# A hybrid decoder layer on one core: sums of weight quarters computed early on VectorE and kept in DRAM, weight units of four blocks

## The chip, the cores and the metric

The kernel runs on one core of a Trainium2 chip. The metric is the device time of one execution in microseconds; a profile of one further execution shows what every engine did.

## What is computed

One layer of a causal decoder, for 512 prompt rows and 8 x 4 sample rows together (544 token columns, all in float32):

```python
z = rmsnorm(x, g) @ w_in               # 2048 -> 7728: pooling input, queries, keys/values, gates
A = pool_mixer(...); B = nsa(...)      # windowed means; three-branch attention
h = x + rmsnorm(w_out(sigmoid(ga) * A @ w_pool_proj + sigmoid(gb) * B @ w_nsa_proj))
y = h + rmsnorm(ConvFFN(rmsnorm(h)))   # w_up: 2048 -> 2 x 5632, conv + gelu gate, w_down: 5632 -> 2048
```

## The kernel before

All weights lie in DRAM in the order of use, cut into blocks of 128 x 128. `plan()` lists the units: eight blocks each (1024 columns, 512 KB). The class `Weights` streams them. `load` brings a unit into a ring of three raw tiles by a DMA on SP's queue; `split` turns it into a high part (a copy on ScalarE, L227) and a low part (a subtraction on VectorE, L229), two halves of 512 columns each, into rings of three. `unit` (L349 to L351) multiplies: for every block and token half three matmuls of 128 x 128 by 272 columns (high by high, high by low, low by high). After these three it calls `ws.progress`, which emits the split of the unit two ahead at fixed points, and `tick(0.5)`, so a tick is six matmuls. The schedule is manual: each engine and each DMA queue works through its instructions in the order in which this program emits them.

`tick` also drives side work. A generator in `bg` takes `rate` steps per tick; attention (`compress_stage`, `natural_stage`, `sample_stage`, `prompt_stage`) is emitted this way between the matmuls of the input projection. `later` delays single actions by some ticks.

The order of the stages: a first projection of three column blocks; the columns m = 3 to 20 (keys, values, queries; background rate 0.7); 30 gate columns (rate 1.0) beside attention; the pooling columns; the merge, in which for each of 16 m the products `pp` and `np` are multiplied with gates read back from DRAM (`sg_d`); the output projection `wo`, at whose end the normalised state is formed; then the feed-forward part.

The up projection of the feed-forward part is a 2 x 2 block product in seven multiplications. Its weight matrix has four quarters per column block j (44 of these): quarters 0 and 1 belong to one row of the 2 x 2 scheme, 2 and 3 to the other. A first stage (`p`, L1383) does two of the seven products and stores them in `stash_d`. The second, called the sum stage here, does five per j: four need the sums s1 = q2 + q3, s2 = s1 - q0, s3 = q0 - q2, s4 = q1 - s2 as weights, one needs q3 itself. GpSimd computes the four sums per j (`weight_sum`, L1335, 128 x 1024 each), driven by `hooks` of the weight stream which also fetch the quarters (`quarter`, L205). The sum stage has five evacuations per j on VectorE (L1466 to L1477) and the convolution and gate (`conv`): two steps on VectorE (L1413, L1414), a gelu on ScalarE (L1415), the product with the value half on VectorE (L1418, L1419) and a store of `act_d` (L1422). The products t2 and t3 use one PSUM bank one after the other: t3 may begin once L1466 has read t2. The down projection (`dn`) follows in seven chunks.

Evacuations in the input projection use two PSUM banks, one for each token half (`pair(..., 0)`).

Of the kernel before, what the change touches and what calls it, by code (L numbers as in the profile page):

```python
# [40 lines left out]
KH = KT // 2  # L41

# [9 lines left out]
def kinner(mat, m, kts=None, halves=BOTH):  # L52
    kts = list(range(KT) if kts is None else kts)
    return [(tuple((mat, k, m) for k in kts[i:i + 8]), halves) for i in range(0, len(kts), 8)]


def kouter(mat, ms):
    return [(tuple((mat, k + i, m) for i in range(2) for m in ms), BOTH) for k in range(0, KT, 2)]


def grp(gs):
    return [(tuple(("grp%d" % g, k, m) for g in gs for m in range(2) for k in range(2)), BOTH)]


def plan():
    u = kouter("in", [0, 1, 2])
    for m in range(3, 21):
        u += kinner("in", m)
    for m in GATES[:30]:
        u += kinner("in", m)  # L70
    for m in range(8):
        u += kinner("in", M_POOL + m)
        if m == 6:
            u += grp((0, 1))
    for m in GATES[30:]:
        u += kinner("in", m)
    u += grp((2, 3))
    for m in range(KT + 1):
        if m < KT:
            u += kinner("pp", m, range(8))  # L80
        if m:
            u += kinner("np", m - 1, range(8))
    for m in range(KT - NSPLIT):
        u += kinner("out", m)
    for h in BOTH:
        for m in range(KT - NSPLIT, KT):
            u += kinner("out", m, halves=(h,))
    for j in range(0, FT, 2):
        u += [(quad(i, q), (0,)) for q in (0, 1) for i in (j, j + 1)]
    for j in range(FT):  # L90
        u += [(quad(j, q), (0,)) for q in ("s2", "s1", "s3", 3, "s4")]
    for a, b in CHUNKS:
        if b - a == 8:
            for m in range(KT):
                u += kinner("dn", m, range(a, b))
        else:
            for hs in (BOTH,) if b < FT else ((0,), (1,)):
                for m in range(0, KT, 2):
                    u += [(tuple(("dn", k, m + i) for i in range(2) for k in range(a, b)), hs)]
    return u  # L100


def quad(j, q):


    if isinstance(q, str):
        return tuple((q, k, j) for k in range(KH))
    return tuple(("up", q % 2 * KH + k, (FT if q < 2 else 0) + j) for k in range(KH))


def computed(b):
    return b[0][0][0] == "s"


def stored(units):
    return [b for b, _ in units if not computed(b)] + [quad(j, 2) for j in range(FT)]
# [58 lines left out]
class Weights:  # L175


    RAW, PARTS = 3, 3

    def __init__(self, nc, pool, dram, units):  # L180
        self.nc, self.pool, self.dram, self.units = nc, pool, dram, units
        self.i = self.nd = self.ns = 0
        self.raw, self.done = {}, {}
        self.ahead, self.depth = 1, 1
        self.off, _ = offsets(units)
        self.kept, self.again = {}, {}
        self.given, self.hooks = set(), {}
# [4 lines left out]
    def load(self, n):  # L192
        while self.nd < min(n, len(self.units)):
            if self.nd in self.again or self.nd in self.given:
# [3 lines left out]
            t = self.pool.tile([P, 1024], F32, name=f"wr{i}", tag="wraw", bufs=self.RAW)  # L198
            self.fetch(t, self.units[i][0])
            self.raw[i] = t  # L200
            self.nd += 1

    def fetch(self, t, blocks):
        w, o = len(blocks) * P, self.off[blocks]
        self.nc.sync.dma_start(t[:, :w], self.dram[o:o + P * w].rearrange("(p c) -> p c", c=w))  # L205

    def split(self, i, part):

        if i in self.again:
            if part == 0:  # L210
                self.done[i] = self.kept[self.again[i]]
            elif part == 3:
                self.ns = i + 1
            return
        if part == 0 and i in self.kept:
            self.load(i + 1)
            self.done[i] = self.kept[i]
        elif part == 0:
            self.load(i + 1)
            self.done[i] = (self.pool.tile([P, 1024], F32R, name=f"wh{i}", tag="whi", bufs=self.PARTS),  # L220
                            self.pool.tile([P, 1024], F32R, name=f"wl{i}", tag="wlo", bufs=self.PARTS))
        hi, lo = self.done[i]
        w = self.width(i)
        c = slice(0, w // 2) if part < 2 else slice(w // 2, w)
        raw = self.raw[i]
        if part % 2 == 0:
# [3 lines left out]
        if part == 3:  # L230
# [3 lines left out]
    def finish(self, i):  # L234
        while self.ns <= i:
            for part in range(4):
                self.split(self.ns, part)

    def get(self):
# [3 lines left out]
        for f in self.hooks.pop(i, ()):  # L243
            f()
        self.load(i + 1 + self.depth)
        return self.units[i] + self.done.pop(i)

    def progress(self, n, total):
# [3 lines left out]
        at = [max(1, total // 8), 3 * total // 8, total // 2, 3 * total // 4]  # L252
        if n in at:
# [4 lines left out]
            if part == 3:  # L258
                self.load(self.i + 1 + self.depth)
# [3 lines left out]
def layer(ctx: ExitStack, tc: tile.TileContext, a: dict):  # L263
# [16 lines left out]
    wp, wp_es = pool("weights", "left")  # L280
    up, up_es = pool("u", "left")
# [3 lines left out]
    ws = Weights(nc, wp, a["wst"], plan())  # L285
# [19 lines left out]
    bg = {"gen": None, "credit": 0.0, "rate": 0.0}  # L305
    deferred = []

    def tick(x=1.0):
# [4 lines left out]
        if bg["gen"] is None:  # L313
            return
        bg["credit"] += bg["rate"] * x
        while bg["credit"] >= 1.0 and bg["gen"] is not None:
            bg["credit"] -= 1.0
            if next(bg["gen"], "end") == "end":
                bg["gen"] = None

    def drain():
        while bg["gen"] is not None:
            if next(bg["gen"], "end") == "end":
                bg["gen"] = None
        while deferred:
            deferred.pop(0)[1]()

# [37 lines left out]
    def full(mat, m, ps, X, done=None):  # L365
        for _ in range(2):
# [89 lines left out]
    for k in range(0, KT, 2):  # L456
# [3 lines left out]
        ws.load(k // 2 + 2)  # L460
# [12 lines left out]
        if k == KT - 2:  # L473
            ws.ahead, ws.depth = 2, ws.RAW
            ws.finish(9)
# [3 lines left out]
        unit(lambda mat, m: psA[m], U, lambda k: k == 0, lambda k: k == KT - 1, byk=True)  # L479
# [633 lines left out]
    def grp_unit(gs):  # L1113
# [19 lines left out]
        unit(psof, X, lambda k: k == 0, lambda k: k == 1, done)  # L1133
# [44 lines left out]
    for m in range(KT + 1):  # L1178
        if m < KT:
            ga = gates[m][0]  # L1180
            p1 = pair(f"pp{m}", 2 * m)
            unit(lambda *_: p1, AX_, lambda k: k == 0, lambda k: k == 7, lambda m, h: V.scalar_tensor_tensor(
                ga[:, HS[h]], ga[:, HS[h]], 1.0, p1[h], OP.add, OP.mult))
        if m:
            ga, gb = gates.pop(m - 1)
            p2 = pair(f"np{m - 1}", 2 * m + 1)
            unit(lambda *_: p2, OX, lambda k: k == 0, lambda k: k == 7, lambda m, h: V.scalar_tensor_tensor(
                gb[:, HS[h]], gb[:, HS[h]], 1.0, p2[h], OP.add, OP.mult))
# [8 lines left out]

    v0p, v0_es = pool("v0", "right")
# [114 lines left out]
    drain()  # L1313
    mg_es.close()

    GE = 2 + SEQ + NB * 6
    ffn, raws = {}, {}
    first_sum = ws.i + 2 * FT

    def open_ffn():  # L1320
# [6 lines left out]
        ffn["fw"], ffn["fw_es"] = pool("quarters", "left")  # L1327

    def quarter(j, q, bufs=1):
        t = raws[j, q] = ffn["fw"].tile([P, 1024], F32, name=f"wq{q}_{j}", tag=f"q{q}", bufs=bufs)  # L1330
        ws.fetch(t, quad(j, q))
# [5 lines left out]
    def hook(i, f):  # L1337
        ws.hooks.setdefault(i, []).append(f)

    def give(j, b):  # L1340


        def fetch():
            quarter(j, 3, 2)
            quarter(j, 2)
            quarter(j, 0)
            ws.raw[b + 3] = raws[j, 3]

        def s1():
            weight_sum(j, "s1", 2, 3, OP.add)  # L1350
            ws.raw[b + 1] = raws[j, "s1"]

        def s2():
            weight_sum(j, "s2", "s1", 0, OP.subtract)
            ws.raw[b] = raws[j, "s2"]
            quarter(j, 1)

        def s3():
            weight_sum(j, "s3", 0, 2, OP.subtract)
            ws.raw[b + 2] = raws[j, "s3"]  # L1360

        def s4():
            weight_sum(j, "s4", 1, "s2", OP.subtract)
            ws.raw[b + 4] = raws[j, "s4"]

        for x, f in ((-6, fetch), (-4, s1), (-3, s2), (-2, s3), (0, s4)):
            hook(b + x, f)
        ws.given.update(range(b, b + 5))

    for j in range(FT):  # L1370
        give(j, first_sum + 5 * j)
# [3 lines left out]
    for j in range(0, FT, 2):  # L1375
        pa = [psp.tile([P, 512], F32, name=f"p1_{i}", tag=t, bufs=2)[:, :H2] for i, t in ((j, "g"), (j + 1, "tr"))]
        st = {}
        for q in range(2):
            for i in range(2):
                unit(lambda *_: [pa[i]], VX, lambda k: k == 0, lambda k: k % KH == KH - 1, skip=True)  # L1380
# [72 lines left out]
    for j in range(FT):  # L1453
# [3 lines left out]
        def product(ps, form, start):  # L1457
            xh, xl = forms[form]
            unit(lambda *_: [ps], lambda mat, k, h: (xh[:, k % KH, :], xl[:, k % KH, :]),
                 lambda k: start and k % KH == 0, lambda k: k % KH == KH - 1, skip=True)  # L1460
# [24 lines left out]
    ffn["fw_es"].close()  # L1485
# [42 lines left out]
    for ci, (c0, c1) in enumerate(CHUNKS):  # L1528
        first, last = (lambda k: k == c0), (lambda k: k == c1 - 1)
        if ci + 1 < len(CHUNKS):  # L1530
# [8 lines left out]
            step = 1 if c1 - c0 == 8 else 2  # L1539
            for m0 in range(0, KT, step):  # L1540
                pss = {m: nextpair(f"dn{ci}_{m}") for m in range(m0, m0 + step)}
                unit(lambda mat, m: pss[m], DX, first, last, done)
# [7 lines left out]
        for n in range(2, 8):  # L1550
            i = ws.i + n
            ws.kept[i] = tuple(kp.tile([P, 1024], F32R, name=f"k{t}{n}") for t in "hl")
            ws.again[i + 8] = i
        for h in range(2):
            for m0 in range(0, KT, 2):
                pss = {m: bank(f"dn{h}_{m}", m, h) for m in (m0, m0 + 1)}
# [25 lines left out]
    y_es.close()  # L1582
    ps_es.close()
# [95 lines left out]
```

## Time and profile before

| | |
|---|---|
| time, median of 3 runs | 3064.67 us (3063.96 to 3066.19) |
| the profiled execution | 3064.26 us, span of its instructions 3062.6 us |
| busy: TensorE, VectorE, ScalarE, GpSimd | 2906.9, 1962.4, 1101.6, 694.9 us |
| moved by DMA | 431.06 MB, 141 GB/s on average |

Busy time is the sum over an engine's instructions, with overlaps counted once. Matmuls are pipelined, so TensorE's rate is better read from the number of matmuls in a stretch than from its busy time. A DMA's time to landing runs from its issue to its last byte; issuing alone takes the queue about 0.4 us.

### The profile page before, as it was taken

Reading aid. Unit: us, or ns where it says so; the run is one execution under the profiler, and the core shown is the slowest. Engines: PE = TensorE matmul, PEld = TensorE weight load, DVE = VectorE, ACT = ScalarE, POOL = GpSimd, SP = SyncE. Lnnn points to the kernel's source line nnn. Section 1 sums busy time; section 2 is a strip of 40 time slices with the busy share of each in tenths; the row PEclk is TensorE's granted clock in tenths of the full one; section 3 lists DMA queues with packets and bytes.
Section 4 is the critical chain, followed back from the end, with each engine's and each line's share of the span. In section 5 each row is a group of like instructions: output and inputs, shape, how many; then the busy total and the mean of one; then the engine's idle time right before and its main releaser. Section 6 shows DMA issues by size and latency. Waiting matters only on the chain.

```text
span 3062.6 us, 56964 instructions
## 1 busy us (share of the span) xinstructions
PE 2906.9 (95%) x22799; PEld 2811.3 (92%) x22799; DVE 1962.4 (64%) x3353; ACT 1101.6 (36%) x2345; POOL 694.9 (23%) x576
## 2 busy tenths in 40 slices
PE   9799999999999999998999989888888899999996
PEld 9798889999999999997999988888888899999996
DVE  7232435777755544258774899999999973444347
ACT  4111224444432322245564443343444343222223
POOL 4232220000003000112100555555555520000004
PEclk9899999999999999999999999999999999999998
DMA  6542564222225443256766544444444443333234
GB/s 207 134 134 98 194 230 147 68 74 77 78 71 99 132 136 127 87 160 192 260 224 232 177 140 150 156 149 140 140 155 156 147 161 118 108 111 111 97 103 150
DMA packets 185288, 431.06 MB, mean 141 GB/s; under 512 B 39611, under 2 KB 77916, under 8 KB 185022
## 3 DMA queue, kind: packets, MB, share of 16 engines
q1 hardware_dynamic: 161240, 395.94, 38.8%
q10 hardware_dynamic: 16614, 14.68, 2.2%
q0 software_dynamic: 7168, 16.79, 1.8%
q8 instruction: 179, 2.93, 0.4%
q14 instruction: 87, 0.71, 0.1%
HBM read 369.23 MB, written 58.11 MB: 140 GB/s over the span
## 4 chain that ended last, share of the span: by engine, by line
PE 73%; DVE 17%; issue 5%; DMA 2%; ACT 1%; POOL 0%; SPq 0%; DVEq 0%; ACTq 0%; POOLq 0%
DVE wl L229 8%; PE in L349 7%; PE in L351 7%; PE in L350 6%; PE dn L351 5%; PE dn L349 5%; PE dn L350 5%; DVE cv L1413 4%; PE p L349 3%; PE p L351 3%; PE p L350 3%; PE wo L351 2%; PE wo L349 2%; PE wo L350 2%; PE oa L990 1%
## 5 line engine op out<-in xcount | busy, mean ns | idle before, releaser
L229 DVE TENSOR_TENSOR wl<-wr,wh 128x512 fp32r<-128x512 f32 (+1 forms) x756 | 542.5, 730 | 327.6 <-ACT wh L227 318.5
L227 ACT CAST wh<-wr 128x512 fp32r<-128x512 f32 (+1 forms) x756 | 439.4, 616 | 790.7 <-PE dn L350 329.5
L349 PE MATMUL in<-uh,wh 128*128 128x272 f32 x1600 | 490.5, 307 | 0.0
L351 PE MATMUL in<-uh,wl 128*128 128x272 f32 x1600 | 462.6, 289 | 0.0
L350 PE MATMUL in<-ul,wh 128*128 128x272 f32 x1600 | 461.5, 288 | 0.0
L351 PE MATMUL dn<-h,wl 128*128 128x272 f32 x1312 | 379.6, 289 | 0.0
L349 PE MATMUL dn<-h,wh 128*128 128x272 f32 x1312 | 378.3, 288 | 0.7 <-ACT y L1535 0.4
L229 DVE TENSOR_TENSOR wl<-ws,wh 128x512 fp32r<-128x512 f32 x352 | 375.0, 1094 | 4.9 <-ACT wh L227 3.4
L350 PE MATMUL dn<-l,wh 128*128 128x272 f32 x1312 | 377.2, 288 | 0.0
L349 PEld LDWEIGHTS in<-uh,wh 128*128 128x128 f32 x1600 | 302.2, 189 | 39.0 <-issue 37.9
L1335 POOL TENSOR_TENSOR ws<-wq,wq 128x1024 f32<-128x1024 f32 x88 | 225.1, 2557 | 349.3 <-PE p L351 207.2
L350 PEld LDWEIGHTS in<-ul,wh 128*128 128x128 f32 x1600 | 303.3, 190 | 0.7
L351 PEld LDWEIGHTS in<-uh,wl 128*128 128x128 f32 x1600 | 301.9, 189 | 0.2 <-DVE wl L229 0.2
L227 ACT CAST wh<-ws 128x512 fp32r<-128x512 f32 x352 | 205.5, 620 | 256.0 <-PE ug L350 94.8
L349 PEld LDWEIGHTS dn<-h,wh 128*128 128x128 f32 x1312 | 247.0, 188 | 1.1 <-ACT y L1535 0.6
L350 PEld LDWEIGHTS dn<-l,wh 128*128 128x128 f32 x1312 | 247.3, 188 | 0.0
L351 PEld LDWEIGHTS dn<-h,wl 128*128 128x128 f32 x1312 | 246.6, 188 | 0.0
L1537 DVE TENSOR_TENSOR y<-y,dn 128x272 f32<-128x272 f32 x160 | 70.1, 438 | 247.9 <-PE dn L351 247.9
L349 PE MATMUL p<-vh,wh 128*128 128x272 f32 x704 | 204.5, 290 | 0.8 <-ACT st L1383 0.8
L351 PE MATMUL p<-vh,wl 128*128 128x272 f32 x704 | 203.7, 289 | 0.0
L350 PE MATMUL p<-vl,wh 128*128 128x272 f32 x704 | 202.7, 288 | 0.0
L349 PE MATMUL ug<-t3h,wh 128*128 128x272 f32 x352 | 116.4, 331 | 90.3 <-DVE sl L1466 86.9
(355 smaller groups left out, 7667.5 us busy)
## 6 DMA issues: line engine op xcount, KB each, us to landing
wr<-wst SPq DMA_DIRECT2D x376, 512.0 KB, 3.5
wq<-wst SPq DMA_DIRECT2D x176, 512.0 KB, 4.6
stash_d<-st SPq DMA_DIRECT2D x44, 272.0 KB, 3.1
act_d<-val SPq DMA_DIRECT2D x44, 272.0 KB, 2.2
ar<-act_d SPq DMA_DIRECT2D x44, 272.0 KB, 3.1
sg_d<-gz SPq DMA_DIRECT2D x32, 272.0 KB, 2.1
X<-cache POOLq DMA_DIRECT2D x128, 64.0 KB, 2.8
sl<-stash_d SPq DMA_DIRECT2D x44, 136.0 KB, 4.0
```

The source lines that it names most:

```text
L227: self.nc.scalar.copy(hi[:, c], raw[:, c])
L229: self.nc.vector.tensor_tensor(lo[:, c], raw[:, c], hi.bitcast(F32)[:, c], OP.subtract)
L349: T.matmul(ps, wh, xh, start=first(k), stop=False, skip_group_check=skip)
L350: T.matmul(ps, wh, xl, start=False, stop=False, skip_group_check=skip)
L351: T.matmul(ps, wl, xh, start=False, stop=last(k), skip_group_check=skip)
L990: T.matmul(oacc[g][pl, qt * P:(qt + 1) * P], VN[:, br, kt, pr * P + par * 64:pr * P + par * 64 + 64], st[i][1][par][:, kt * P:(kt + 1) * P ...
L1335: G.tensor_tensor(t, raws[j, x], raws[j, y], op)
L1413: V.scalar_tensor_tensor(c[:, :n], g[:, 1:n + 1], cw[:, j, 1:2], c[:, :n], OP.mult, OP.add)
L1537: V.tensor_tensor(y[:, m, HS[h]], y[:, m, HS[h]], pss[m][h], OP.add)
```

## The change

The weight sums leave the sum stage. A new generator `sum_stage` is driven by `tick` through a second slot, `side`, beside `bg`. For each j and each half of K it loads four quarters of four blocks (128 x 4 x 512, 1 MiB) into a tile `su` of two buffers, makes four VectorE operations of 128 x 512 in place, and stores the tile into a DRAM buffer `sums_d`; both DMAs go through SP's queue. One turn takes nine steps and there are 88 turns. The rate is 0.75 steps per tick from m = 3 on, 0.5 from the start of the sample stage and 0.78 from the end of the prompt stage. The sum stage then loads s1 to s4 as ordinary weight units from `sums_d`. Hooks, `quarter`, `weight_sum` and the GpSimd work are gone.

A weight unit has now four blocks (512 columns, 256 KB) and is split by one copy and one subtraction. Units of one output are in sequence, so all four (before: two) units of an m run through both token halves. The ring of raw tiles and of parts has three units each at first and grows after the merge and after the output projection to six each (`grow`). The splits are then emitted three, four and five units ahead instead of two.

```diff
+UB = 4
+UW = UB * P
...
-    return [(tuple((mat, k, m) for k in kts[i:i + 8]), halves) for i in range(0, len(kts), 8)]
+    return [(tuple((mat, k, m) for k in kts[i:i + UB]), halves) for i in range(0, len(kts), UB)]
...
-    RAW, PARTS = 3, 3
...
+    def grow(self, pool, raws, parts):
...
+            if b[0][0] in SLOT:
+                self.nc.sync.dma_start(t, self.sums[b[0][2], b[0][1] // UB][:, SLOT[b[0][0]], :])
+            else:
+                o = self.off[b]
+                self.nc.sync.dma_start(t[:, :w], self.dram[o:o + P * w].rearrange("(p c) -> p c", c=w))
...
-        for f in self.hooks.pop(i, ()):
-            f()
-        self.load(i + 1 + self.depth)
+        self.load(i + self.ahead + self.raws - 1)
...
-        at = [max(1, total // 8), 3 * total // 8, total // 2, 3 * total // 4]
+        at = [max(1, total // 4), total // 2]
...
+    ws = Weights(nc, a["wst"], sums_d, plan())
+    ws.grow(wp, 3, 3)
...
+        for b in (bg, side):
+            if b["gen"] is None:
+                continue
+            b["credit"] += b["rate"] * x
+            while b["credit"] >= 1.0 and b["gen"] is not None:
+                b["credit"] -= 1.0
+                if next(b["gen"], "end") == "end":
+                    b["gen"] = None
...
+    def sum_stage():
+
+        for j in range(FT):
+            for c in range(KH // UB):
+                t = sup.tile([P, 4, UW], F32, name=f"su{j}_{c}", tag="su", bufs=2)
+                o = ws.off[quad(j, 0)[c]]
+                nc.sync.dma_start(t, a["wst"][o:o + 4 * P * UW].rearrange("(q p c) -> p q c", q=4, c=UW))
+                for _ in range(3):
+                    yield
+                a11, a12, a21, a22 = [t[:, q, :] for q in range(4)]
+                V.tensor_tensor(a22, a21, a22, OP.add)
+                yield
+                V.tensor_tensor(a21, a11, a21, OP.subtract)
+                yield
+                V.tensor_tensor(a11, a22, a11, OP.subtract)
+                yield
+                V.tensor_tensor(a12, a12, a11, OP.subtract)
+                yield
+                yield
+                nc.sync.dma_start(sums_d[j, c], t)
+                yield
...
+        side["rate"] = 0.5
         yield from sample_stage()
         s2_es.close()
         yield from prompt_stage()
+        side["rate"] = 0.78
...
+    side["gen"], side["rate"] = sum_stage(), 0.75
...
+    ws.grow(w1p, 2, 1)
+    ws.ahead, ws.raws = 3, 5
...
+    drain(side)
...
+    ws.grow(w2p, 1, 2)
...
-    def weight_sum(j, n, x, y, op):
-        t = raws[j, n] = ffn["fw"].tile([P, 1024], F32, name=f"w{n}_{j}", tag="sum", bufs=3)
-        G.tensor_tensor(t, raws[j, x], raws[j, y], op)
...
+                if (j, q) == (0, 0):
+                    ws.ahead, ws.raws = 4 + i, 6
```

## Rows read from the trace of the kernel before

**Rows 1.** The page's 40 slices of the span: busy tenths of TensorE and VectorE.

```profile
PE   9799999999999999998999989888888899999996
DVE  7232435777755544258774899999999973444347
```

**Rows 2.** Stages: us; PE, PEld, DVE, ACT, POOL busy (x count); clock, DMA share, GB/s.

```profile
55.00:318.00 263.00, 245.97 (x1876) 225.47 (x1875) 76.35 (x216) 41.13 (x72) 68.71 (x128) 0.96 0.45 131
318.00:891.00 573.00, 573.00 (x4801) 515.96 (x4800) 355.16 (x956) 229.19 (x605) 42.17 (x75) 1.00 0.36 120
891.00:1217.00 326.00, 326.00 (x2597) 326.00 (x2596) 160.06 (x295) 90.15 (x161) 32.09 (x27) 1.00 0.44 122
...
1434.00:1702.00 268.00, 267.20 (x2116) 266.82 (x2116) 177.44 (x300) 145.50 (x322) 23.19 (x19) 1.00 0.72 239
1702.00:2498.00 796.00, 705.38 (x5282) 695.43 (x5281) 772.84 (x878) 324.88 (x662) 430.41 (x217) 0.96 0.43 149
2498.00:2988.00 490.00, 489.64 (x3894) 489.42 (x3893) 204.35 (x373) 128.62 (x243) 0.78 (x1) 1.00 0.34 114
```

**Rows 3.** VectorE's costliest groups, 1702 to 2498 us: shapes, count | busy, mean ns.

```profile
L229 DVE TENSOR_TENSOR wl<-ws,wh 128x512 fp32r<-128x512 f32 x348 | 372.4, 1098 | 3.7 <-ACT wh L227 2.2
L1418 DVE TENSOR_TENSOR val<-val,cv 128x512 f32<-128x512 f32 x43 | 118.5, 2755 | 0.0
L1413 DVE SCALAR_TENSOR_TENSOR cv<-ge,cw,cv 128x560 f32<-128x560 f32 x43 | 117.3, 2727 | 0.0
L229 DVE TENSOR_TENSOR wl<-wq,wh 128x512 fp32r<-128x512 f32 x88 | 57.9, 696 | 0.0
L1414 DVE SCALAR_TENSOR_TENSOR cv<-ge,cw,cv 128x560 f32<-128x560 f32 x43 | 38.5, 895 | 1.5
```

**Rows 4.** Timeline of VectorE and GpSimd near 2009 us: start, us, engine, operation.

```profile
2009.63 2.75 DVE L229 TENSOR_TENSOR wl<-ws,wh 128x512 fp32r<-128x512 f32 x1
...
2009.43 2.39 POOL L1335 TENSOR_TENSOR ws<-wq,ws 128x1024 f32<-128x1024 f32 x1 [2.81 <-issue]
```

**Rows 5.** TensorE's waits, 1702 to 2498 us, then 60 to 1220 us: total, times, longest.

```profile
PE ug L349 <- DVE sl L1466: 86.9, 42, 2.7
...
PE pscb L548 <- DMA ohc<-c_ohc: 17.0, 1, 17.0
```

**Rows 6.** Matmul groups of the input projection, 55 to 318.8 us and 318.8 to 891 us.

```profile
L349 PE MATMUL in<-uh,wh 128*128 128x272 f32 x526 | 155.6, 296 | 0.0
...
L351 PE MATMUL in<-uh,wl 128*128 128x272 f32 x995 | 286.6, 288 | 0.0
```

**Rows 7.** Line L724, GpSimd's first instruction of the sample stage.

```profile
L724 POOL MEMSET qS<- x1: 527/527/527, 318.8 to 318.8; 128x512 f32 x1
```

**Rows 8.** SP's DMA queue near 357 us: start, us to issue, line, transfer.

```profile
348.74 1.30 SPq L713 DMA_DIRECT2D okT<-kw  x2
357.10 0.40 SPq L692 DMA_DIRECT2D kw<-kwT  x1
```

**Rows 9.** Single microseconds after that load's issue, columns as in rows 2.

```profile
357.00:358.00 1.00, 1.00 (x10) 0.84 (x10) 0.47 (x2) 0.42 (x1) 0.58 (x1) 1.00 0.13 41
358.00:359.00 1.00, 1.00 (x13) 0.80 (x13) 0.00 (x0) 0.98 (x3) 0.51 (x2) 1.00 1.03 156
...
361.00:362.00 1.00, 1.00 (x10) 1.00 (x9) 0.97 (x5) 0.00 (x0) 0.70 (x1) 1.00 1.04 422
```

**Rows 10.** DMA issues of the page: transfer, engine, count, size, median us to landing.

```profile
wr<-wst SPq DMA_DIRECT2D x376, 512.0 KB, 3.5
...
sg_d<-gz SPq DMA_DIRECT2D x32, 272.0 KB, 2.1
```

**Rows 11.** SP's waits in the whole span: total, times, longest.

```profile
SPq L703 <- DMA ov<-vw: 20.7, 5, 8.4
...
SPq L692 <- DMA okT<-kw: 19.4, 3, 8.3
```

**Rows 12.** Timeline of ScalarE near 96 us: start, us, operation [idle before, releaser].

```profile
96.19 0.62 ACT L227 CAST wh<-wr 128x512 fp32r<-128x512 f32 x1 [12.28 <-DMA wr<-wst]
```

More of the change, by code (lines that the diff above doesn't have):

```diff
@@ L106, in quad @@
     if isinstance(q, str):
[L107 to L112, printed above, removed]
+        b = [(q, k, j) for k in range(KH)]
+    else:
+        b = [("up", q % 2 * KH + k, (FT if q < 2 else 0) + j) for k in range(KH)]
+    return [tuple(b[c:c + UB]) for c in range(0, KH, UB)]
+SLOT = {"s2": 0, "s4": 1, "s3": 2, "s1": 3}
 def stored(units):
-    return [b for b, _ in units if not computed(b)] + [quad(j, 2) for j in range(FT)]
+    return ([quad(j, q)[c] for j in range(FT) for c in range(KH // UB) for q in range(4)]
+            + [b for b, _ in units if b[0][0] not in SLOT])
 def offsets(units):
@@ L235, in finish @@
         while self.ns <= i:
-            for part in range(4):
+            for part in range(2):
                 self.split(self.ns, part)
@@ L280, in layer @@
     wp, wp_es = pool("weights", "left")
+    sup, su_es = pool("sums", "left")
     up, up_es = pool("u", "left")
@@ L312, in tick, with drain @@
             deferred.pop(0)[1]()
[L313 to L324, printed above, removed]
+        for b in (bg, side):
[6 more added lines that the diff above has]
+                    b["gen"] = None
+    def drain(b=bg):
+        while b["gen"] is not None:
+            if next(b["gen"], "end") == "end":
+                b["gen"] = None
         while deferred:
             deferred.pop(0)[1]()
+    def sum_stage():
[18 more added lines that the diff above has]
+                yield
     def later(n, fn):
@@ L365, in full @@
     def full(mat, m, ps, X, done=None):
-        for _ in range(2):
+        for _ in range(KT // UB):
             unit(lambda *_: ps, X, lambda k: k == 0, lambda k: k == KT - 1, done)
@@ L473, in layer @@
         if k == KT - 2:
-            ws.ahead, ws.depth = 2, ws.RAW
-            ws.finish(9)
+            ws.ahead, ws.raws = 2, 3
+            ws.finish(k + 2)
             for h in range(2):
@@ L478, in layer @@
             tick(0)
-        unit(lambda mat, m: psA[m], U, lambda k: k == 0, lambda k: k == KT - 1, byk=True)
+        for _ in range(2):
+            unit(lambda mat, m: psA[m], U, lambda k: k == 0, lambda k: k == KT - 1, byk=True)
     ident = const_tiles["c_id"]
@@ L1131, in done @@
             V.scalar_tensor_tensor(Al[:, o, HS[h]], ps[h], sc_, Ah.bitcast(F32)[:, o, HS[h]], OP.mult, OP.subtract)
-        unit(psof, X, lambda k: k == 0, lambda k: k == 1, done)
+        for _ in gs:
+            unit(psof, X, lambda k: k == 0, lambda k: k == 1, done)
     for m in range(8):
@@ L1458, in product @@
             xh, xl = forms[form]
-            unit(lambda *_: [ps], lambda mat, k, h: (xh[:, k % KH, :], xl[:, k % KH, :]),
-                 lambda k: start and k % KH == 0, lambda k: k % KH == KH - 1, skip=True)
+            for _ in range(KH // UB):
+                unit(lambda *_: [ps], lambda mat, k, h: (xh[:, k % KH, :], xl[:, k % KH, :]),
+                     lambda k: start and k % KH == 0, lambda k: k % KH == KH - 1, skip=True)
         st, g = stash.pop(j), ge[j]
@@ L1537, in done @@
                     V.tensor_tensor(y[:, m, HS[h]], y[:, m, HS[h]], pss[m][h], OP.add)
[L1539 to L1542, printed above, removed]
+            for m in range(KT):
+                pss = {m: nextpair(f"dn{ci}_{m}")}
+                for _ in range((c1 - c0) // UB):
+                    unit(lambda mat, m: pss[m], DX, first, last, done)
             drain()
```

141 lines of the change are left out of this document (62 added, 79 removed).

## The prediction, made before the result was known

> **What bounds the kernel now.** I read the slices first. TensorE is at nine tenths nearly everywhere; only the sum stage, where VectorE shows nines, has it at eight [rows 1]. The table by stage makes that exact [rows 2]. The down projection does 3894 matmuls in 490 us, 125.8 ns each, at full clock. The sum stage needs 44 x 5 x 8 x 3 = 5280, which at that pace is 664 us; it takes 796, with VectorE busy for 773 and a granted clock of 0.96. So 132 us are lost there. The groups say why [rows 3]: subtractions that read a computed sum take 1098 ns on average, those that read a fetched quarter 696; the gate product and the first convolution step take over 2.7 us. The timeline shows one such case: a VectorE operation begins during a 2.39 us GpSimd sum and lasts 2.75 us, to the end of the next one's start, instead of 0.7 [rows 4]. TensorE then waits 86.9 us in 42 waits for L1466 [rows 5]. From 60 to 1220 us it has one wait worth a row, 17.0 us on a constant [rows 5]: these stages are bound by TensorE, and VectorE has room there, 29% busy in the projection, 62% beside attention, 49% in the pooling and merge stretch [rows 2].
>
> **What the change takes away: the GpSimd sums.** VectorE's work in the sum stage without contention is 772.8 less 348 x (1.098 - 0.696) = 140, less 43 x (2.755 - 0.696) = 89 (taking the gate product like a subtraction of its shape), less 43 x (2.727 - 0.895) = 79: 465 us, for 664 of TensorE [rows 2, 3]. That is 70%, and t3 begins a whole product (24 matmuls, 3.0 us) after t2 ends, so one waiting operation no longer shows. The stage becomes TensorE's, 664 us; I leave 3 us for single waits: **-129 us**. The ends are 0 gained on half of the waits (-65) and -132. A fifth quarter per j to load adds 23 MB; with it the stage moves 149 x 796 / 664 + 35 = 214 GB/s, less than the 239 of the first up stage, where TensorE ran through [rows 2].
>
> **What it adds: 88 turns of `sum_stage`.** Steps first. Matmuls of the projection, three lines of 526 up to the sample stage's start at 318.8 us, are 263 ticks; at 0.75 that is 197 steps, 21.9 turns, one per 12.0 us [rows 6, 7]. Then 995 x 3 / 6 = 498 ticks at 0.5 give 27.6 turns, one per 20.7 us [rows 6]. The 2597 matmuls from 891 to 1217 us are 433 ticks, at 0.78 some 37.5 turns, one per **8.7 us** [rows 2]. Sum 784 of 792 steps, so the work does end about with the merge.
>
> Now a turn's own length. The load of turn n stands on SP's queue behind the store of turn n-1, which waits for that turn's fourth operation; two buffers do not help, as the order of emission holds the load back. The first operation of turn n waits on VectorE for this load, and all later evacuations and splits stand behind it. So a turn lasts at least L + b: L from the fourth operation to the landing of the next load, b from the first operation to the fourth.
>
> b is 4 x 0.70 = 2.8 us [rows 3] and the other VectorE work of the three steps between. In the last stretch these are a third of 8.7 us at 49% busy, 1.4 us: b = 4.2.
>
> L is not in the trace; I bound it. Store issue to load issue is 0.4 us [rows 8]. Fixed time from issue to landing: a 272 KB store lands after 2.1, a 512 KB load after 3.5 us [rows 10]; at 375 GB/s their bytes take 0.7 and 1.4, which leaves 1.4 to 2.1. A 1 MB load issued at 357.10 shows the lag: the DMA engines are at 0.13 in the microsecond of the issue and full in the next, with a best microsecond of 422 GB/s [rows 8, 9]; over long stretches full engines would carry 239 / 0.72 = 332 [rows 2]. Store and load together are 2.1 MB, 5.0 to 6.3 us. If the load runs behind the store: L = 0.4 + 1.7 + 5.6 + 0.3 (a weight unit between) = **8.0**. Low end, a load that is not held up by the store: 0.4 + 1.4 + 2.5 = 4.3. High end: 0.4 + 2.1 + 6.3 + 0.7 = 9.5. I take 8.0: both transfers go through one queue over the same engines, and the rows show these filled by 1 MB.
>
> The Trainium skill ("DMA: Bandwidth & Descriptors", Queues, rings and completion order) says that each engine consumes descriptors in ring order, though a later one may finish first; no run here shows a 1 MB pair.
>
> - Pooling and merge: 8.0 + 4.2 = 12.2 us against 8.7, 3.5 x 37.5 = **+131 us**. Splits are emitted two units (6 us) ahead; that delays a first stall, but not the pace of a turn which is longer than its matmuls. Ends: 4.3 + 4.2 = 8.5, nothing; 13.7, +188.
> - Projection: b = 2.8 + a third of 12.0 us at 29% = 4.0; with L = 8.0 the turn is 12.0, just TensorE's time. But the weights are already late near 96 us, ScalarE waits 12.28 us for one [rows 12], and an evacuation now has 12 matmuls (1.5 us) until its bank is needed, before 24, so a blocked VectorE shows at once. Low end 0 (added work can't gain); high end L = 12.3 throughout, 4.3 x 21.9 = 94. I take **+25**, as the lateness stands in the first turns only.
> - Beside attention: a turn has 20.7 us and needs 8.0 + 2.8 + a third of 20.7 at 62% (4.3) = 15.1. Nothing by that; but SP waits there for stores to land, 20.7 and 19.4 us in 8 waits [rows 11], and a sum load behind one comes late. 0 to +40, I take **+10**.
> - Smaller units: about 550 more loads of 0.4 us issue each [rows 8], 220 us of a queue that is mostly idle; 256 KB is asked for some 8 us ahead and 512 KB lands after 3.5 [rows 10]. 0; if this cover goes, each late unit costs the difference, and the output projection's one-half units, 1.5 us each, would show it first (to +20). The eight left steps: 0.
>
> Sum against the profiled execution: 3064.3 - 129 + 131 + 25 + 10 = 3101; the median shown is 0.4 us higher, so **3101 us**.
>
> **The rivals.**
>
> *The turn is hidden.* The load is not held up by the store (L = 4.3), and VectorE has room in every stage before the output projection [rows 2]. Then 8.5 is under 8.7, and only some 15 us of late loads remain: 3064 - 129 + 15 = 2950. For it: best microseconds of 422 GB/s [rows 9] and DMA shares of 0.36 to 0.45 in the three stretches [rows 2]. Against it: 2.1 MB per 8.7 us are 241 GB/s on top of 122, 363 together, more than any long stretch shows. It decides from L = 4.5; between 4.5 and 6.9 the kernel still ends faster, since a turn of 11.1 us costs 90. This is the other side, with 0.34.
>
> *The sum stage gains half.* With GpSimd gone the chain ge, convolution, gelu, gate product could still hold VectorE, so -65 instead of -129: 3165. Against it stands the 70%. 0.10.
>
> *A megabyte takes longer than the rows suggest.* The turn would then be set by two slow transfers, and the time would be well above 3101. The rows speak against it: 422 GB/s in a microsecond and a start lag of about one [rows 9]. If each transfer took 6 us, L would be 14, the turn 18, and the stages +350 and +130: over 3400. 0.03. The Trainium skill (same page, Bandwidth) gives 6.15 us for 1 MB, measured on GpSimd's queue; by it this rival would be the forecast.
>
> That the sums are not done in time, so that the change doesn't do what it says, is excluded by the count of steps.
>
> **How the numbers follow.** The forecast's case (turn longer than its matmuls) has 0.53, with its own range 3050 to 3150: the last stretch from +90 to +165, the projection 0 to +50. Of it 0.45 is slower by over 0.2% (6 us, about what a measurement can tell from no change), 0.04 within, 0.04 faster. The hidden turn gives 0.32 faster and 0.02 within; the other two 0.13 slower. Together: faster 0.36, same 0.06, slower 0.58. For 8 in 10 the range has to take in most of the hidden turn's case: 2955 to 3160.
>
> **What would show it.** Right: the sum stage lasts about 665 us with subtractions at 0.7 us and full clock; the stretch from pooling to merge takes some 450 us instead of 326; there, the first operation of each turn waits 3 to 5 us for the load of `su`, TensorE waits for splits or evacuations about once a turn, and `su` loads land some 7 us after issue. Wrong: a stretch that stays near 326 us with `su` loads landing in under 5 us (the hidden turn); TensorE waits in the sum stage (the half gain); or a loss mainly beside attention, where I put only 10 us.

## The result and the profile after

The changed kernel takes 3392.36 us (median of 4 runs, 3386.43 to 3405.63) against 3065.43 before: a ratio of 1.1072, 95% interval 1.1039 to 1.1105. The direction was forecast; the size was not, and 3392 lies far outside 2955 to 3160.

The page's slices after, busy tenths of TensorE and VectorE and the clock granted to TensorE, answer to [rows 1]:

```profile
PE   7678787899999676767798999999999999999995
DVE  5333343388786444444437875677777774444456
PEclk9789898899999878888899999999999999999998
```

The weak stretch has changed places: the sum stage, now in the slices from the 26th on, is at nine, and TensorE is at six to eight in the first eight slices and in the middle. VectorE is at three to five tenths in those slices, so neither engine is full there.

The same table by stage as [rows 2], after the change (first stage, projection, sample attention, prompt attention, pooling and merge, output projection, sum stage, rest):

```profile
0.00:73.40 73.40, 53.86 (x340) 49.70 (x340) 41.01 (x47) 32.48 (x56) 22.92 (x23) 0.93 0.39 123
73.40:434.90 361.50, 272.87 (x1904) 250.19 (x1905) 131.56 (x305) 43.98 (x72) 69.07 (x131) 0.86 0.71 224
434.90:683.10 248.20, 200.13 (x1579) 166.67 (x1579) 91.63 (x250) 51.93 (x124) 42.05 (x74) 0.89 0.73 245
683.10:1084.40 401.30, 394.13 (x3216) 362.61 (x3215) 330.63 (x819) 179.98 (x482) 0.12 (x1) 1.00 0.49 166
1084.40:1648.20 563.80, 398.24 (x2595) 386.40 (x2593) 250.18 (x442) 91.05 (x161) 31.63 (x27) 0.83 0.64 207
1648.20:1877.90 229.70, 205.12 (x1541) 198.63 (x1542) 122.01 (x201) 83.65 (x164) 37.65 (x44) 0.96 0.48 142
...
2146.60:2817.10 670.50, 666.58 (x5281) 665.97 (x5281) 484.40 (x878) 341.44 (x662) 4.25 (x44) 1.00 0.69 212
2817.10:3390.80 573.70, 538.86 (x4238) 534.27 (x4236) 270.61 (x467) 164.25 (x305) 34.69 (x41) 0.98 0.39 117
```

Stages of the kernel before that [rows 2] does not show by themselves, in the same columns:

```profile
0.00:53.50 53.50, 49.21 (x352) 48.28 (x353) 44.88 (x47) 32.94 (x58) 25.29 (x21) 0.97 0.54 188
53.50:318.80 265.30, 248.27 (x1894) 227.76 (x1893) 78.26 (x221) 41.13 (x72) 69.41 (x133) 0.96 0.45 129
318.80:500.50 181.70, 181.70 (x1572) 154.13 (x1571) 66.67 (x208) 49.47 (x122) 42.04 (x74) 1.00 0.65 217
500.50:890.70 390.20, 390.20 (x3222) 360.73 (x3222) 288.04 (x748) 179.43 (x484) 0.03 (x1) 1.00 0.22 75
890.70:1216.50 325.80, 325.80 (x2595) 325.80 (x2594) 159.84 (x294) 90.45 (x161) 32.18 (x28) 1.00 0.44 122
1216.50:1433.80 217.30, 201.44 (x1541) 197.74 (x1540) 116.09 (x196) 80.36 (x163) 37.58 (x44) 0.97 0.42 134
```

In the order of the stages the difference is +20, +96, +67, +11, +238, +12, 0 in the first up stage, -126 in the sum stage, +9 in the rest: +328 us of span. The pooling and merge stretch has 2595 matmuls in both kernels and takes 326 and 564 us: of the 238 us TensorE is idle for 166, and busy for 72 more on the same matmuls.

What VectorE waits for, first in the whole span, then in the pooling and merge stretch alone (total, times, longest):

```profile
DVE su L355 <- DMA su<-wst: 496.6, 66, 23.2
```

```profile
DVE su L355 <- DMA su<-wst: 248.3, 34, 11.9
```

What became of the transfers, from the DMA issues of the page (count, size, median us to landing; the medians are over the landings that the trace holds, 11 of the loads and 12 of the stores):

```profile
su<-wst SPq DMA_DIRECT2D x88, 1024.0 KB, 8.2
sums_d<-su SPq DMA_DIRECT2D x88, 1024.0 KB, 5.7
```

VectorE stands idle 497 us before the first side operations of 66 of the 88 turns; in the pooling and merge stretch it is 7.3 us a time. TensorE's waits for splits there come to 150 us in 41 waits, about one a turn. One turn in the merge, first on VectorE, then on SP's queue (start, us, operation):

```profile
1403.59 0.69 DVE L361 TENSOR_TENSOR su<-su 128x512 f32<-128x512 f32 x1
...
1414.08 0.69 DVE L355 TENSOR_TENSOR su<-su 128x512 f32<-128x512 f32 x1 [7.90 <-DMA su<-wst]
...
1419.27 0.68 DVE L361 TENSOR_TENSOR su<-su 128x512 f32<-128x512 f32 x1
...
1432.06 0.69 DVE L355 TENSOR_TENSOR su<-su 128x512 f32<-128x512 f32 x1 [9.12 <-DMA su<-wst]
```

```profile
1404.91 0.33 SPq L220 DMA_DIRECT2D wr<-wst  x1
1405.29 0.42 SPq L364 DMA_DIRECT2D sums_d<-su  x1
1405.77 0.42 SPq L351 DMA_DIRECT2D su<-wst  x1
...
1422.05 0.47 SPq L364 DMA_DIRECT2D sums_d<-su  x1
```

The fourth operation (L361) ends at 1404.28; a weight load stands on SP's queue before the store; store and load go out at 1405.29 and 1405.77; the load lands 8.3 us later, at 1414.08; four operations and what is between take until 1419.95. In the prediction's terms that is L = 9.8 and b = 5.9 us. Over the 37 turns that begin in this stretch (from the starts and ends of L355, L361, L364 and L351 in the trace) L averages 11.0 and b 4.3 us: 1.2 from the fourth operation to the store, 1.0 from the store to the load, 8.8 from the load's issue to the next first operation.

Meanwhile TensorE runs out of split weights. Its clock in three stretches of the same turn (columns as above):

```profile
1402.00:1404.00 2.00, 0.00 (x0) 0.00 (x0) 1.90 (x4) 0.62 (x1) 0.00 (x0) 1.00 0.00 0
1405.00:1407.00 2.00, 2.00 (x9) 2.00 (x10) 1.18 (x3) 0.00 (x0) 0.00 (x0) 0.50 0.55 113
...
1409.00:1412.00 3.00, 3.00 (x26) 3.00 (x26) 0.00 (x0) 0.00 (x0) 0.00 (x0) 1.00 0.92 310
```

After standing still it starts again at 0.50 of its speed, that is 1.2 GHz, and does 9 matmuls in 2 us; later in the turn, at 1.00, it does 26 in 3. Over the stretch the granted clock averages 0.83.

The sum stage went as forecast. Its groups on VectorE, against [rows 3], and TensorE's one row of waits there, against [rows 5]:

```profile
L244 DVE TENSOR_TENSOR wl<-wr,wh 128x512 fp32r<-128x512 f32 x441 | 300.3, 690 | 133.3 <-ACT wh L242 79.8 <-PE uqk L389 48.7
L1424 DVE SCALAR_TENSOR_TENSOR cv<-ge,cw,cv 128x560 f32<-128x560 f32 x43 | 34.5, 802 | 1.5
...
L1428 DVE TENSOR_TENSOR val<-val,cv 128x512 f32<-128x512 f32 x43 | 29.4, 685 | 0.0
```

```profile
PE ug L388 <- DVE sl L1477: 3.9, 3, 2.1
```

The gate product takes 685 ns instead of 2755, the subtractions 690 instead of 1098, and 83 of the 86.9 us of waits for L1466 (now L1477) are gone. VectorE is busy for 484 of 670 us where it was busy for 773 of 796. The splits are also emitted further ahead in this stage than before; no run separates that from the absence of GpSimd's sums.

### The profile page after: what moved, and what is told of

It reads as the page before. It is cut to its first block, busy times and chain, and to the rows that moved or that the text cites. A ratio compares the mean times of both kernels' runs of the same rounds, so it can differ in the third digit from the quotient of the medians.

```text
span 3390.8 us, 59951 instructions
## 1 busy us (share of the span) xinstructions
PE 2997.7 (88%) x22799; PEld 2881.7 (85%) x22799; DVE 1898.1 (56%) x3708; ACT 1142.5 (34%) x2348; POOL 258.0 (8%) x400
## 4 chain that ended last, share of the span: by engine, by line
PE 63%; DMA 18%; DVE 11%; issue 4%; ACT 2%; SPq 2%; ACTq 0%; POOL 0%; DVEq 0%; POOLq 0%
DMA su<-wst 15%; PE dn L388 5%; PE dn L390 5%; PE dn L389 5%; PE in L388 4%; PE in L390 3%; PE in L389 3%; DVE wl L244 3%; PE ug L388 3%; PE uqk L389 3%; PE ug L389 3%; PE uqk L388 3%; PE ug L390 3%; PE uqk L390 3%; PE p L388 2%
## 5 line engine op out<-in xcount | busy, mean ns | idle before, releaser
L242 ACT CAST wh<-wr 128x512 fp32r<-128x512 f32 (+1 forms) x1202 | 728.0, 617 | 1331.6 <-PE in L389 364.4
L244 DVE TENSOR_TENSOR wl<-wr,wh 128x512 fp32r<-128x512 f32 (+1 forms) x1202 | 841.4, 707 | 564.1 <-ACT wh L242 497.7
L388 PE MATMUL in<-uh,wh 128*128 128x272 f32 x1600 | 510.1, 319 | 101.2 <-DVE gz L1088 31.2
L389 PE MATMUL in<-ul,wh 128*128 128x272 f32 x1600 | 477.0, 298 | 0.0
L355 DVE TENSOR_TENSOR su<-su 128x512 f32<-128x512 f32 x88 | 60.8, 691 | 527.5 <-DMA su<-wst 496.6
L389 PEld LDWEIGHTS in<-ul,wh 128*128 128x128 f32 x1600 | 319.0, 199 | 0.7
L388 PE MATMUL wo<-mh,wh 128*128 128x272 f32 x512 | 150.9, 295 | 12.3 <-DVE gb L1233 7.1
L390 PE MATMUL wo<-mh,wl 128*128 128x272 f32 x512 | 151.0, 295 | 8.5 <-DVE wl L244 8.5
L389 PE MATMUL wo<-ml,wh 128*128 128x272 f32 x512 | 148.8, 291 | 0.0
L388 PEld LDWEIGHTS p<-vh,wh 128*128 128x128 f32 x704 | 132.6, 188 | 1.4 <-ACT st L1393 1.4
```

Source lines behind the costliest of these rows:

```text
L242: self.nc.scalar.copy(hi[:, c], raw[:, c])
L244: self.nc.vector.tensor_tensor(lo[:, c], raw[:, c], hi.bitcast(F32)[:, c], OP.subtract)
L355: V.tensor_tensor(a22, a21, a22, OP.add)
L388: T.matmul(ps, wh, xh, start=first(k), stop=False, skip_group_check=skip)
L389: T.matmul(ps, wh, xl, start=False, stop=False, skip_group_check=skip)
L390: T.matmul(ps, wl, xh, start=False, stop=last(k), skip_group_check=skip)
```

## The experiments

The runs up to the half rate are one execution each. Four executions of the changed kernel differ by 19 us, so differences of a few microseconds between single runs say nothing.

**Without the side work, and with its operations alone.** In the first, the sum stage loads plain quarters and the generator is not started; in the second, the 352 operations come back on a tile that stays in SBUF.

```diff
-    side["gen"], side["rate"] = sum_stage(), 0.75
+    side["gen"], side["rate"] = None, 0.75
```

> The changed kernel without its side work: no sums are formed, the sum stage loads unsummed quarters in their place (so the sums are left out), everything else as in the change. Theory (the loss up to the merge comes from the side turns, whose length is set by the load behind the store): the stretch from the pooling columns to the end of the merge is back at 326 us from 563, the projection at 265 from 362, the sum stage stays at 670; in all 3392 - 237 - 97 - 65 - 12 = about 2980 us. Rival (the smaller units and shorter ring cost the time, through evacuations that have half the slack): most of the loss stays, over 3200 us. What is left of the first stage's 19 us, the output projection's 13 and the tail's 9 belongs to the units in either case.

```diff
+        z = sup.tile([P, UW], F32, name="suz")
...
-                V.tensor_tensor(a22, a21, a22, OP.add)
-                yield
...
-                nc.sync.dma_start(sums_d[j, c], t)
-                yield
+                for _ in range(4):
+                    V.tensor_tensor(z, z, z, OP.add)
+                    yield
```

> As the run without side work, with the 352 side operations of VectorE (128 x 512, on a tile that stays in SBUF) put back at their steps, but none of the side loads and stores; the sums are left out. Theory: VectorE has room for them, within 15 us of the run without side work. Rival (VectorE's load is what stretches the stages up to the merge): at least 100 us above it, most of it in the pooling and merge stretch.

Measured: 2986.06 and 2989.31 us (before, on the same chip, 3063.53). The first run's first stage, its pooling and merge stretch and its sum stage, then the second run's pooling and merge stretch:

```profile
0.00:75.10 75.10, 56.34 (x340) 53.00 (x340) 41.09 (x47) 32.62 (x56) 22.94 (x24) 0.89 0.38 120
...
928.10:1253.10 325.00, 325.00 (x2594) 324.99 (x2593) 156.95 (x294) 93.99 (x161) 32.14 (x27) 1.00 0.45 121
...
1742.10:2409.90 667.80, 666.44 (x5283) 666.03 (x5282) 484.43 (x878) 341.71 (x662) 4.24 (x44) 1.00 0.69 213
```

```profile
929.60:1256.00 326.40, 326.38 (x2594) 325.29 (x2593) 262.10 (x444) 93.00 (x161) 33.21 (x27) 1.00 0.45 121
```

So of the changed kernel's span the side work is 3390.8 - 2984.4 = 406 us, and its VectorE time 3, as good as nothing. The change's gain without any side work is 78 us, not 126: the smaller units and their shorter ring cost about 50, of which 20 are in the first stage, 10 in the rest and 10 beside the sample attention.

**The same traffic without the ties.**

```diff
-                V.tensor_tensor(a22, a21, a22, OP.add)
+                V.tensor_tensor(z, z, z, OP.add)
...
-                nc.sync.dma_start(sums_d[j, c], t)
+                nc.sync.dma_start(sums_d[j, c], r1[:, None, :UW].to_broadcast([P, 4, UW]))
```

> The same bytes by the same queue at the same steps and the same number of VectorE operations, but untied: the operations use a tile that stays in SBUF, the stores write a constant row block, so no operation waits for a load and no store for an operation; the sums are left out. Theory (the waits of the chain load, four operations, store set the pace): the pooling and merge stretch falls from 563 to at most 380 us, in all below 3080 us. Rival (the DMA engines are simply full, 363 GB/s asked for): the stretch stays above 480 us, in all above 3250 us.

Measured: 3121.08 us; pooling and merge:

```profile
998.10:1385.00 386.90, 352.90 (x2595) 342.70 (x2593) 259.91 (x443) 92.34 (x161) 31.54 (x27) 0.95 0.90 301
```

This lies between the two, much nearer to the theory, whose bounds (380 and 3080) it misses by 7 and 41 us. By spans the traffic alone costs 3119.4 - 2987.7 = 132 us, the ties 3390.8 - 3119.4 = 271. By stages the traffic costs 61 us from pooling to merge, 35 in the projection and 31 beside the sample attention, the ties 177, 58 and 26. The DMA engines are 90% busy here and 64% in the changed kernel: tied, they wait for VectorE as VectorE waits for them.

**The load issued earlier.** First with turns of half the width and four buffers, then with the change's own width and two buffers, so that only the order differs.

```diff
+                t = tiles[n] = sup.tile([P, 4, W2], F32, name=f"su{n}", tag="su", bufs=4)
...
             V.tensor_tensor(a21, a11, a21, OP.subtract)
+            fetch(n + 2)
```

> The whole computation, with the side work cut into 176 turns of half the width (128 x 4 x 256, four buffers) and each load issued about one and a half turns before its first operation, at the same rates. Theory: the load no longer stands between two turns, VectorE waits for it less than 100 us in all (497 in the change), and the time lies between 2960 and 3120 us. Rival (full DMA engines, or SP's queue held up by waits on stores and splits): above 3250 us.

```diff
             V.tensor_tensor(a21, a11, a21, OP.subtract)
+            fetch(n + 1)
```

> The changed kernel with turns of full width, two buffers and the same rates; only the load of turn n+1 is issued eight steps ahead of its first operation, behind the second operation of turn n, instead of three steps ahead and behind the store of turn n. Theory (the place of the load behind the store stretches the turn): VectorE's wait for the load falls from 497 to below 200 us and the time to 3100 to 3200 us; the width of the turns matters less. Rival (the width and the four buffers of the early-load kernel made the gain): above 3300 us.

Measured: 3101.68 and 3155.71 us. Pooling and merge and VectorE's wait for the load in the first, then in the second:

```profile
989.80:1365.90 376.10, 345.57 (x2595) 337.11 (x2593) 284.05 (x595) 92.87 (x161) 28.70 (x27) 0.97 0.99 311
...
DVE su L365 <- DMA su<-wst: 35.4, 18, 7.1
```

```profile
996.30:1414.90 418.60, 360.11 (x2594) 349.31 (x2592) 251.73 (x442) 92.45 (x161) 30.66 (x27) 0.93 0.83 275
...
DVE su L363 <- DMA su<-wst: 153.9, 45, 11.1
```

Moving one load in the order of emission, and nothing else, gives back 3392 - 3156 = 237 us: 145 from pooling to merge, 48 in the projection, 36 beside the sample attention. So most of the 271 us of the ties comes from the place of the load behind the store; 154 of the 497 us of VectorE's wait are left. Both runs came out as their theories said. With the wait nearly gone in the first run, the DMA engines are at 0.99.

**Half the rate in the last stretch.**

```diff
-        side["rate"] = 0.78
+        side["rate"] = 0.39
```

> The changed kernel with 0.39 instead of 0.78 steps per tick from the pooling columns on; what is not done by the end of the output projection is emitted there in one piece. Theory (a turn has a length of its own of about 15 us): with 17.4 us of matmuls per turn the turn is hidden, the pooling and merge stretch falls from 563 to at most 350 us, while some eight turns in one piece at the end cost about 100 us; in all 3220 to 3300 us. Rival (each side operation delays TensorE by itself, so the loss goes with the number of turns): half the loss stays, 440 us or more in that stretch.

Measured: 3289.73 us, and

```profile
1084.60:1455.10 370.50, 341.91 (x2595) 335.10 (x2593) 208.86 (x371) 91.56 (x161) 32.33 (x27) 0.97 0.69 210
```

193 of 238 us return with half the turns, where a cost per operation would have given back half. The stretch is 20 us above the expected 350: VectorE still waits for the load there, 76 us in 15 waits; what else adds to it is open. The turns that were left go out in one piece in the first up stage, which takes 357 us instead of 268.

These turns show the chain with almost nothing beside it, since TensorE stands still. One of them, on VectorE and on SP's queue:

```profile
1709.92 0.69 DVE L361 TENSOR_TENSOR su<-su 128x512 f32<-128x512 f32 x1
1718.35 0.69 DVE L355 TENSOR_TENSOR su<-su 128x512 f32<-128x512 f32 x1 [7.74 <-DMA su<-wst]
```

```profile
1710.64 0.33 SPq L364 DMA_DIRECT2D sums_d<-su  x1
1711.06 0.39 SPq L351 DMA_DIRECT2D su<-wst  x1
```

The store goes out as the fourth operation ends, the load 0.4 us later, and the next first operation begins 7.3 us after that. Over the seven turns from 1697 us on L is 7.7, b 2.9 and the turn 10.6 us.

**The work spread by other rates.** The kernels from here on stand on the early load with turns of half the width and four buffers.

```diff
-    side["gen"], side["rate"] = sum_stage(), 0.75
+    side["gen"], side["rate"] = sum_stage(), 0.5
...
-        side["rate"] = 0.5
+        side["rate"] = 0.3
         yield from sample_stage()
         s2_es.close()
+        side["rate"] = 0.7
         yield from prompt_stage()
-        side["rate"] = 0.78
+        side["rate"] = 0.5
...
     ws.ahead, ws.raws = 3, 5
+    side["rate"] = 0.6
```

> The early-load kernel (whole computation) with the same 88 turns' worth of work spread by other rates: 0.5 in the projection, 0.3 beside the sample attention, 0.7 beside the prompt attention, 0.5 from the pooling columns to the merge, 0.6 in the output projection. Theory (with the wait of the chain gone, what is left up to the merge, about 120 us over the run without side work, is full DMA engines: 0.83, 0.86 and 0.99 busy in three stretches at the old rates, 0.51 beside the prompt): asked for less than the engines carry everywhere, the pooling and merge stretch falls from 376 to at most 340 us, and the time to 3010 to 3050, under the kernel before. Rival (the rest is VectorE's, or SP's order): the time stays within 30 us of 3102.

Measured: 3064.66 us, ratio 1.0 (0.9991 to 1.001): even with the kernel before, 15 us above the theory's upper bound. Pooling and merge, and the first up stage:

```profile
968.00:1305.50 337.50, 330.16 (x2594) 327.96 (x2592) 239.89 (x486) 93.54 (x161) 29.98 (x27) 0.99 0.86 265
...
1534.80:1814.50 279.70, 270.09 (x2118) 269.26 (x2117) 181.77 (x314) 154.28 (x324) 15.40 (x16) 0.98 0.78 241
```

The stretch fell as expected; the first up stage is 11 us longer, with 13 more VectorE operations in it: some turns were left over and emitted in one piece.

**The first stage, in three tries.** A split two units ahead, fewer weight loads ahead (`ws.load(k + 3)`), and last the rows of x four ahead of their use (together with the second set of rates below).

```diff
-        self.ahead, self.raws = 1, 2
+        self.ahead, self.raws = 2, 2
```

> As the spread run, with the splits of the first stage emitted two units ahead instead of one. Theory (the first stage lost about 20 us because a unit of three blocks is split only 18 matmuls ahead, before 36): the first stage falls from 74 towards 55 us, and the time by 10 to 20 us against the spread run. Rival (that stage waits for loads or ScalarE's other work): no change within 5 us.

> The spread run with one edit in the first stage: the weights are asked for three units ahead instead of four, so that the fourth load, which finds no free tile in a ring of three, no longer stands on SP's queue before the next rows of x. Theory (the first stage lost 20 us because x comes late: ScalarE waits 28.6 us for x there, before 5.2): that stage falls from 75 to at most 62 us and the time by 10 to 20 us, under the kernel before. Rival (x is late for the smaller transfers themselves): within 4 us of the spread run.

```diff
-        if k + 2 < KT:
-            load_x(k + 2)
-            load_x(k + 3)
+        if k + 4 < KT:
+            load_x(k + 4)
+            load_x(k + 5)
```

> The run with the second set of rates, with one edit in the first stage: the rows of x are asked for four ahead of their use instead of two (the six buffers allow it). The run with the first loads mended changed nothing, and SP still waited 54 us for splits there with the loads of x behind. Theory (x stands behind weight loads that wait for a tile of the short ring): ScalarE's wait for x falls from 29 us to under 8, the first stage from 74 to at most 62 us, and the time by 10 to 18 us, to about 3048. Rival (ScalarE and VectorE are the bound of that stage with smaller units): the stage stays above 70 us.

Measured: 3064.01 us (ratio to before 1.0002, 0.9992 to 1.0011) and 3065.26 (0.9998, 0.9989 to 1.0007), no change against the spread run in either: two theories fell. The third: 3040.88 us, ratio 0.9922 (0.9909 to 0.9936). Its first stage, and ScalarE's wait for x in the first 75 us:

```profile
0.00:55.40 55.40, 48.98 (x340) 47.01 (x340) 42.78 (x46) 32.45 (x56) 24.79 (x23) 0.94 0.51 163
...
ACT uh L473 <- DMA x<-xT: 3.0, 4, 1.3
```

The wait was 28.6 us in the changed kernel. The short ring makes SP wait for splits, and x stood behind it.

**Two more sets of rates.** In the order of the stages 0.35, 0.1, 0.85, 0.65, 0.45 (this also carries the second try above), and with x ahead 0.3, 0.1, 0.95, 0.47, 0.75.

> As the run with the first loads mended, with the side work moved further to where the DMA engines have room: 0.35 in the projection, 0.1 beside the sample attention, 0.85 beside the prompt attention, 0.65 from pooling to merge, 0.45 in the output projection. Theory (what is left is the share of the DMA engines asked for; VectorE, 89% busy beside the prompt at 0.7, still has room): 8 to 20 us below the run with the first loads mended, 3020 to 3045 us. Rival (VectorE becomes the bound beside the prompt): that stretch grows from 402 to over 425 us and the time is no lower.

> As the run with x ahead, with a third set of rates: 0.3 in the projection, 0.1 beside the sample attention, 0.95 beside the prompt attention, 0.47 from pooling to merge, 0.75 in the output projection, so that no turn is left over for the first up stage. Theory (what the side work costs goes with the DMA share asked for, 0.95 in the pooling and merge stretch at 0.65, and the left-over turns delay the first up stage by 11 us): the pooling and merge stretch falls from 353 to 338 us or less, the first up stage from 281 to 270, and the time to 3005 to 3030 us. Rival (VectorE, at 0.95 beside the prompt, or the output projection's chain takes it back): within 8 us of the run with x ahead.

Measured: 3061.66 us (0.9992, 0.9983 to 1.0001), a few us and not the 8 to 20 expected; its pooling and merge stretch at 0.65 took 353 us with the DMA engines at 0.95, while the stretch beside the prompt stayed at 402, so the rival's reason did not hold either. Then **3032.08 us, ratio 0.9894 (0.9879 to 0.991)**, faster than both kernels; prompt attention, pooling and merge, output projection and first up stage:

```profile
527.70:943.20 415.50, 398.91 (x3217) 364.56 (x3217) 383.65 (x1015) 185.13 (x482) 0.12 (x1) 0.99 0.74 238
943.20:1278.50 335.30, 328.46 (x2594) 326.67 (x2593) 235.45 (x475) 93.28 (x161) 29.93 (x27) 0.99 0.85 258
1278.50:1511.10 232.60, 209.55 (x1541) 203.46 (x1542) 183.75 (x364) 83.83 (x164) 37.53 (x44) 0.94 0.95 315
1511.10:1781.20 270.10, 268.19 (x2118) 267.38 (x2117) 177.39 (x303) 154.41 (x324) 15.77 (x16) 1.00 0.79 241
```

The left-over turns are gone and the merge is down by 20 us against the run with x ahead, the output projection is up by 6 and the stretch beside the prompt by 12, where VectorE is now busy for 384 of 416 us. By the medians 9 us are gained, the time is just above the expected 3030, and the rival, which said up to 8, is only just missed. Not tried: more room for the ring in the last stage, which stays some 10 us longer than before.

## Why the prediction was wrong

*The sum stage* was right: -126 us for -129, with the durations and the vanished wait it named. Of the rivals, half the gain fell here. (In [rows 4] the slow operation ends at 2012.38, 0.56 us after the end of the sum shown beside it.)

*The turn* was right as a mechanism: it lasts L + b, VectorE waits for the load about once a turn, and the order of emission is most of why (the run with the order alone). Its size was off: forecast 8.0 + 4.2 = 12.2 us, measured 11.0 + 4.3 = 15.3 over the 37 turns, or 563.8 / 37.5 = 15.0 by the stretch. So b was right, and **the term that failed is L**. Its own parts were not wrong: 0.4 + 1.7 + 5.6 = 7.7 is what a turn takes with nothing beside it (the turns in one piece, 7.7 us), although the 375 GB/s in it stands in no row: it lies between the 422 of a row and the 332 worked out from one. What failed is the step from there to a turn beside the matmuls, for which the sum has 0.3 us, a weight unit between. I counted from the fourth operation straight to the store. In 26 of the 37 turns other DMAs stand there on SP's queue, nearly all weight loads, which wait until a split frees their tile; in 14 turns such a DMA stands between the store and the load. At the mean that is 1.2 us before the store and 0.6 more than forecast before the load. The load then takes 8.8 us from its issue to the next first operation, not 7.3, with weights and gates on the same DMA engines; which of them costs the 1.5 us is not isolated. About three microseconds times 37.5 turns are the missing 107 us of this stretch. VectorE's wait was 7.3 us a time where I had given 3 to 5 as the sign.

*The projection* was forecast at +25, since a turn of 12.0 us just fitted TensorE's 12.0. It lasted 361.5 / 21.9 = 16.5 us. The step that failed is taking the rows' lateness for the first turns only; L averaged 11.9 us over the whole stretch, near the 12.3 of my high end. *The sample attention* was forecast at +10 with the prompt's; the prompt has +11, the sample +67. A turn of 20.7 us seemed long enough, but I averaged over two stretches. The first has 10.5 turns (42 operations, by the runs without and with them) in its 181.7 us before, 17.3 us each, and already moved 217 GB/s. There L averaged 20.8 us: 5.0 to the store, 5.6 from the store to the load, 10.2 to the next first operation, as SP's queue also carries the attention's transfers and weight loads that wait, 99 us in 25 waits for splits. Of the 67 us about 10 are there without side work, 31 come with its traffic and 26 with the ties.

*The traffic* by itself was put at nothing: the prediction lets it cost time only through L. Untied, it costs 132 us; how much of that is left beside the longer L in the tied kernel is not separated.

*Smaller units* were put at 0; with the shorter ring they cost about 50 us. Some 20 of them are the first stage, which the prediction leaves out: there x is queued behind weight loads that wait (the run with x ahead). The cause of the other 30 is open.

*The hidden turn* fell: L is 7.7 us even with nothing beside the turn, and it decides from 4.5. *The slow megabyte* is right in its premise and wrong in its sum. In the four turns of the pooling and merge stretch whose load went out 3 us or more behind the store, the first operation began 5.8 to 7.2 us after the load's issue, and the stores of the whole run landed after 5.7 us at the median: close to that rival's 6 us each. But the two overlap, 7.7 us for the pair where its L is 14. The measured 3392 lies near its "over 3400" all the same, but with L at 11.0 and not 14.

The range was too narrow even by the prediction's own terms: with the sum stage as forecast and every other term at its high end the sum is 3064 - 129 + 188 + 94 + 40 + 20 = 3277. Pooling and merge, the projection and the attention all came out above their ends, with +238, +96 and +78.

## What to carry to other kernels

A background task that loads, computes and stores through an engine's queue has a period of its own: count it from the last operation to the next load's landing, with everything that stands on the DMA queue between, and compare it with the foreground's time per turn before choosing a rate. Emit the load ahead of the store of the turn before, not behind it; that was worth 237 us here and cost no buffer. When a ring is cut shorter, look at what else shares the queue of its loads, not at the ring's own lead alone.

## What the runs showed of the hardware

The DMA engines carried 311 GB/s over 376 us at a busy share of 0.99, where single microseconds had shown 422 [rows 9]. Stretches in which they were busy for 0.86 and 0.90 were already longer than 326 us (337.5 and 386.9, the second without any tie to a computation). A store and a load of 1 MB, issued 0.4 us apart with almost nothing beside them, were both done 7.7 us after the store's issue. After waits of several microseconds TensorE was granted 1.2 GHz and did 9 matmuls in 2 us, against 26 in 3 us at full clock; what that costs in a turn that VectorE sets was not isolated.
